# First modulation by blocks of 128 columns behind x, and the values projected first, as token rows

## The chip, the cores and the metric

The kernel runs on one core of a Trainium2 chip. The metric is the device time of one execution in microseconds (us). The engines are named as the profile names them: PE is TensorE (matmuls and transposes; PEld its weight loads), DVE is VectorE, ACT is ScalarE, POOL is GpSimd, and SP is SyncE, which only issues DMAs here. Every engine works through its own list of instructions in order and waits for the others by semaphores.

## The reference

One transformer-like block over 1024 latent tokens and 256 context tokens of width 1024, in f32. The part that the change touches is the beginning, cut to what matters:

```
mod   = silu(c)     @ w_ada + b_ada          # shift 1, scale 1, gate 1, shift 2, scale 2, gate 2
mod_c = silu(c_ctx) @ w_ada + b_ada
hc = rmsnorm(ctx, norm1_g) * (1 + csc1) + csh1
k_c, v_c = split(hc @ w_in[:, 512:1536])
h  = rmsnorm(x, norm1_g) * (1 + sc1) + sh1
q, k, v, hv, hx1, hx2, gna, ghy = split(h @ w_in)     # w_in: 1024 x 5120
y_na = neighbourhood_attention(q, k, v, k_c, v_c, rpb)
y_hy = hyena_mixer(hv, hx1, hx2, ...)        # short convolution, two long ones with computed filters
...                                           # gates, output projection, SwiGLU network, last norm
```

## The kernel before

**Products.** A product in f32 is made of three matmuls: each operand is split into a high and a low part (`split`: ScalarE casts the high part, VectorE subtracts), and low x high, high x low and high x high are summed in PSUM (`gemm`). A matmul has 128 contraction rows and streams up to 512 columns into one PSUM bank of 128 partitions.

**Opening** (`hidden`). The columns of `w_ada` for shift 1 and scale 1 (2048 of 6144) are loaded as eight slices of 128 rows, 1 MB each, in turn with x0 to x3 (128 tokens each). Each slice is multiplied as soon as it is there (line 299), with `cs`, the SiLU of c and c_ctx, as stationary operand, 32 columns wide, in the four column groups of PE; all eight accumulate in one bank. Then `ada_early` copies that bank to `msb`, transposes it and adds the biases, which gives scale and shift as columns (`mod1`). Only then can `modulated` work: for each of eight chunks of 128 channels, four transposes of normalised x (line 248), one scaling by `mod1` to `htmp` (ScalarE for even chunks, VectorE for odd ones), and the split to `hTh`, `hTl`. The normalisation (`normed`) takes squares on ScalarE, a square root (`rstd`), a reciprocal and a scaling of the x tiles. A first layer of the Hyena filters' small network (`filter_hidden`, tiles `mlp_ps`, `farg`, `feat`) is computed in the opening too, the second between the two halves of the tokens.

**Input projection** (`project`). The 40 column chunks of `w_in` (128 columns each) are the stationary operand, the transposed h moves: a chunk has two halves of 512 tokens, 24 matmuls each (line 194, tile `in_ps`), and its output has channels on partitions. Chunks 0 to 3 are q, 4 to 7 k, 8 to 11 v, 12 to 23 the Hyena input, 24 to 39 the gates. Chunks 4 to 11 are applied to the context as well (24 matmuls of 256 columns, tile `ctx_ps`). Attention needs the values v with tokens on partitions, so `tokens` transposes chunks 8 to 11 (and 12 to 23) in bank `psc` and stores them. The order is [4, 5] together, so that both run on half 0 while x4 to x7 are made ready, then one chunk after the other.

**What sets the order of work.** Instructions are written out by generators; a scheduler then orders them on each engine by readiness and priority, except for those that are pinned to program order. `_merged` mixes the projection (weight 39) with a side generator (weight `SIDE` = 496) that makes the filters, the remaining modulation rows and the long convolutions. When the side work is over, attention begins: 34 steps, each of which is followed by one half chunk of the projection (24 matmuls) as long as there is one (`left` counts the chunks), and after that by one piece of the Hyena output projection (`hy_ps`, 12 matmuls).

**Buffers.** `hT0` and `hT1` are pools for the transposed h of tokens 0 to 511 and 512 to 1023; the pool `wpool` has two buffers for split weights and one for raw ones; the filter pool `psf` has five PSUM banks; `psg` has two banks in turn, `psc` one. `stg` has two buffers for each kind of staging tile.

## Time and profile before

| what | value |
| --- | --- |
| median of three runs | 1698.57 us (1697.81 to 1703.14) |
| the profiled execution, as timed | 1693.98 us |
| its span in the trace | 1691.6 us |
| first matmul of the input projection | 37.75 us after the span's start |
| attention | about 655 to 908 us |
| PE, share of the span | 97% |
| DVE, ACT, POOL | 73%, 41%, 9% |

The span goes from the first to the last instruction of the trace; the timed execution has 2.4 us around it. The shares are means over the whole span; single stretches differ, the opening most of all. A row of the timeline has start and duration in us, the engine, the line, the operation, output and input tiles, the shape and the number of equal instructions in a row, and in brackets how long the engine had been idle before and what released it. Matmul durations overlap, so that the time from the start of one to the start of the next is what a matmul costs PE.

### The profile page before, as it was taken

Reading aid. Unit: us, or ns where it says so; the run is one execution under the profiler, and the core shown is the slowest. Engines: PE = TensorE matmul, PEld = TensorE weight load, DVE = VectorE, ACT = ScalarE, POOL = GpSimd, SP = SyncE. Lnnn points to the kernel's source line nnn. Section 1 sums busy time; section 2 is a strip of 40 time slices with the busy share of each in tenths; the row PEclk is TensorE's granted clock in tenths of the full one; section 3 lists DMA queues with packets and bytes.
Section 4 is the critical chain, followed back from the end, with each engine's and each line's share of the span. In section 5 each row is a group of like instructions: output and inputs, shape, how many; then the busy total and the mean of one; then the engine's idle time right before and its main releaser. Section 6 shows DMA issues by size and latency. Waiting matters only on the chain.

```text
span 1691.6 us, 22631 instructions
## 1 busy us (share of the span) xinstructions
PE 1645.8 (97%) x8124; PEld 1302.7 (77%) x8124; DVE 1229.1 (73%) x2076; ACT 689.6 (41%) x1206; POOL 153.3 (9%) x274
## 2 busy tenths in 40 slices
PE   6999999999999999999999999999999999999997
PEld 2777667777777787887787887888888888878886
DVE  3799587799986975565866867967865666489467
ACT  4733333222212124545654326733333334355455
POOL 0100210001000022020200001000100111000000
PEclk8999999999999999999999999999999999999999
DMA  9275662655544366344757414333422223395344
GB/s 363 96 241 194 193 215 81 209 168 172 185 169 178 124 204 182 110 140 147 218 159 256 162 62 174 119 129 121 162 92 108 94 102 123 113 359 188 100 119 155
DMA packets 110340, 274.36 MB, mean 162 GB/s; under 512 B 15503, under 2 KB 24595, under 8 KB 107925
## 3 DMA queue, kind: packets, MB, share of 16 engines
q1 hardware_dynamic: 90152, 211.86, 37.3%
q0 software_dynamic: 19280, 60.60, 10.7%
q8 instruction: 64, 1.05, 0.3%
q10 hardware_dynamic: 797, 0.45, 0.1%
q14 instruction: 47, 0.39, 0.1%
HBM read 205.48 MB, written 67.39 MB: 161 GB/s over the span
## 4 chain that ended last, share of the span: by engine, by line
PE 68%; issue 11%; DVE 5%; DMA 3%; ACT 1%; POOL 1%; SPq 0%; DVEq 0%; POOLq 0%; ACTq 0%
PE x_ps L1176 15%; PE in_ps L194 13%; PE z_ps L1176 7%; PE dx_ps L1345 6%; PE out_ps L1114 4%; PE dz_ps L1345 3%; PE dft_ps L447 2%; PE hy_ps L194 2%; PE y_ps L1176 2%; PE pt_ps L805 2%; PE pt_ps L791 2%; PE na_ps L194 2%; PE dy_ps L1345 1%; PE dft_ps L448 1%; PE dft_ps L449 1%
## 5 line engine op out<-in xcount | busy, mean ns | idle before, releaser
L194 PE MATMUL in_ps<-hTh,wl 128*128 128x512 f32 x640 | 258.4, 404 | 0.9 <-ACT proj L619 0.5
L194 PE MATMUL in_ps<-hTl,wh 128*128 128x512 f32 x640 | 252.2, 394 | 0.4 <-DVE hTl L175 0.2
L194 PE MATMUL in_ps<-hTh,wh 128*128 128x512 f32 x640 | 252.2, 394 | 0.0
L194 PEld LDWEIGHTS in_ps<-hTh,wl 128*128 128x128 f32 x640 | 120.5, 188 | 31.3 <-issue 5.3
L194 PEld LDWEIGHTS in_ps<-hTl,wh 128*128 128x128 f32 x640 | 120.6, 188 | 26.5 <-DVE hTl L175 1.9
L194 PEld LDWEIGHTS in_ps<-hTh,wh 128*128 128x128 f32 x640 | 120.5, 188 | 26.6
L175 DVE TENSOR_TENSOR wl<-wr,wh 128x1024 fp32r<-128x1024 f32 (+1 forms) x56 | 59.7, 1067 | 68.4 <-ACT wh L174 68.2
L174 ACT CAST wh<-wr 128x1024 fp32r<-128x1024 f32 (+1 forms) x56 | 51.8, 925 | 139.9 <-PE in_ps L194 112.2
L175 DVE TENSOR_TENSOR ol<-ws,oh 128x512 fp32r<-128x512 f32 x88 | 60.4, 688 | 49.1 <-ACT oh L174 49.0
L175 DVE TENSOR_TENSOR ol<-ar,oh 128x512 fp32r<-128x512 f32 x77 | 52.8, 688 | 48.0 <-ACT oh L174 48.0
L174 ACT CAST oh<-ar 128x512 fp32r<-128x512 f32 x77 | 47.9, 622 | 87.1 <-PE dx_ps L1345 33.1
L174 ACT CAST oh<-ws 128x512 fp32r<-128x512 f32 x88 | 54.7, 622 | 55.7 <-PE x_ps L1176 22.1
L780 ACT ACTIVATE pe<-pe,mx 128x640 f32<-128x640 f32 x64 | 52.6, 823 | 48.7 <-DVE mx L779 48.7
L447 PE MATMUL dft_ps<-a,matf 128*128 128x512 f32 x128 | 66.2, 598 | 4.9 <-issue 2.3
L779 DVE CUSTOM_DVE_ANT_0 pe<-s_ps,bias 128x640 f32<-128x640 f32 x64 | 50.1, 820 | 28.3 <-PE s_ps L774 28.2
L1345 PE MATMUL dx_ps<-ol,oh 128*128 128x512 f32 x176 | 68.7, 390 | 1.7 <-DVE ol L175 1.7
L1345 PE MATMUL dx_ps<-oh,ol 128*128 128x512 f32 x176 | 67.4, 390 | 1.9 <-DVE ol L175 1.9
L1345 PE MATMUL dx_ps<-oh 128*128 128x512 f32 x176 | 68.5, 389 | 0.0
L174 ACT CAST oh<-wr 128x512 fp32r<-128x512 f32 x70 | 43.3, 621 | 51.3 <-PE x_ps L1176 15.5
L175 DVE TENSOR_TENSOR ol<-wr,oh 128x512 fp32r<-128x512 f32 x70 | 48.0, 688 | 22.0 <-ACT oh L174 21.9
L1116 DVE TENSOR_TENSOR x<-x,out_ps 128x512 f32<-128x512 f32 x64 | 42.7, 684 | 16.9 <-PE out_ps L1114 16.7
L895 DVE SCALAR_TENSOR_TENSOR aacc<-wal,cs,aacc 128x512 f32<-128x512 f32 x56 | 41.8, 746 | 17.5 <-DMA wal<-in_w_ada 16.9
(396 smaller groups left out, 4215.8 us busy)
## 6 DMA issues: line engine op xcount, KB each, us to landing
wr<-in_w SPq DMA_DIRECT2D x52, 512.0 KB, 3.4
wr<-in_w_in SPq DMA_DIRECT2D x40, 512.0 KB, 4.4
ar<-g SPq DMA_DIRECT2D x77, 256.0 KB, 3.2
wal<-in_w_ada SPq DMA_DIRECT2D x64, 256.0 KB, 4.1
matf<-in_dft_f SPq DMA_DIRECT2D x32, 384.0 KB, 4.9
bias<-in_rpb SPq DMA_DIRECT2D x64, 192.0 KB, 3.7
g<-t POOLq DMA_DIRECT2D x47, 256.0 KB, 3.1
w<-in_w SPq DMA_DIRECT2D x44, 256.0 KB, 5.4
```

What stands on the lines that cost most here:

```text
L174: self.nc.scalar.copy(hi, src)
L175: self.nc.vector.tensor_sub(lo, src, hi.bitcast(F32))
L194: mm = nc.tensor.matmul(ps, ww[:, k * P:(k + 1) * P], xx[:, k, pos:pos + width], start=(i == 0), stop=(i == n - 1))
L447: nc.tensor.matmul(ps, m[:, 0], v.rearrange("p a b -> p (a b)"), start=True, stop=False)
L779: nc.vector.tensor_tensor_reduce(pe, ps[:, 256:896], bt, -1.0, 3e38, ALU.add, ALU.min, mx[:, 0:1])
L780: nc.scalar.activation(pe, pe, AF.Exp, bias=mx[:, 0:1], scale=-1.0, accum_out=mx[:, 1:2])
L791: pin(nc.tensor.transpose(pt[:, at:at + P], pe[:, c * P:(c + 1) * P], self.ident))
L895: nc.vector.scalar_tensor_tensor(acc, w, c, acc, op0=ALU.mult, op1=ALU.add)
L1114: nc.tensor.matmul(ps, gg[x][:, tk], ww[y][:, sl], start=(i == 0), stop=(i == n - 1))
L1116: nc.vector.tensor_add(x1[:, sl], x1[:, sl], ps)
L1176: mm = nc.tensor.matmul(ps, w[u][:, k * P:(k + 1) * P], x[v][:, k, :], start=(start and k == 0 and i == 0), stop=(stop and k == 3 and i == 2),
L1345: nc.tensor.matmul(ps[j], x[u][:, j * P:(j + 1) * P], w[v], start=(start and i == 0 and c == 0), stop=(stop and i == N - 1 and k == len(re ...
```

## The change

**Modulation by columns.** A new layout of the same columns, `w_ada1`, holds eight blocks; block k has all 1024 rows of the 128 shift columns and the 128 scale columns of chunk k, 1 MB each. `ada_block` multiplies one block (eight matmuls of 32x256 in the four column groups), copies the bank to `msb` (VectorE), sums the four groups with two matmuls against a selector `sel` (which leaves scale and shift as columns without a transpose), and adds the biases. It stands ahead of chunk k of the first half, so that chunk k needs block k alone. The blocks lie in the buffers of the second half's h (`h1`), two to a buffer; the loads are pinned to program order on SP, behind x0 to x3.

**Values first.** Chunks 8 to 11 leave the order; 36 chunks are left, single but for the last two. In their place a new function `opening` in `project` computes v with tokens on partitions: the transposed h is now the stationary operand and 512 columns of v's weights (`wv`, four tiles of two chunks each) move. Four banks (both of `psg`, `psc` and one of `psf`) hold 4 x 128 tokens; each chunk k adds 12 matmuls (line 690 of the changed kernel) once it is there. This is done for tokens 0 to 511, then 512 to 1023, then the 256 of the context (two banks). The banks are copied by ScalarE to `vst` (line 695) and stored. The transposes of v and of the context's v fall away, and so do the context's matmuls of chunks 8 to 11 with 256 columns, in place of which 512-column ones are half as many.

The diff at its core:

```diff
@@ _layout @@
+    out["w_ada1"] = C(A("w_ada")[0, :, :2 * D].reshape(8, P, 2, 8, P).transpose(3, 1, 0, 2, 4)).reshape(8, P, 2048)
+    out["wv"] = C(A("w_in")[0, :, 8 * P:12 * P].reshape(4, 2, P, 512).transpose(0, 2, 1, 3)).reshape(4, P, D)
@@ Block.__init__ @@
-        self.left = 40
+        self.left = 36
@@ ada_early becomes ada_block @@
+    def ada_block(self, pool, psf, w, k, cs, sel):
+        ps = psf.tile([P, 512], F32, tag="f", name="ada_ps")
+        for n in range(8):
+            j = n % 4
+            nc.tensor.matmul(ps[32 * j:32 * j + 32, 0:256], cs[:, n], w[:, n], start=(n < 4), stop=(n >= 4),
+                             tile_position=(0, 32 * j))
+        b = pool.tile([P, 256], F32, tag="msb", name="msb", bufs=2)
+        nc.vector.tensor_copy(b, ps[:, 0:256])
+        for n in range(2):
+            nc.tensor.matmul(ps[:, 256 + 2 * n:258 + 2 * n], b[:, n * P:(n + 1) * P], sel, start=True, stop=True)
+        nc.vector.tensor_scalar(self.mod1[:, :, 1, k], ps[:, 256:258], self.bcol[:, 0, k:k + 1], None, op0=ALU.add)
+        nc.vector.tensor_scalar(self.mod1[:, :, 0, k], ps[:, 258:260], self.bcol[:, 1, k:k + 1],
+                                self.ng[:, 0, k:k + 1], op0=ALU.add, op1=ALU.mult)
@@ hidden @@
+        for j in range(4):
+            load(j)
+        def block(k):
+            if k % 2 == 0:
+                w = h1.tile([P, 2, 8, 256], F32, tag="hTl" if k % 4 else "hTh", name="wada")
+                blocks.extend((w[:, 0], w[:, 1]))
+            inorder(nc.sync.dma_start(blocks[k].rearrange("p a b -> p (a b)"), a["w_ada1"][k]))
+        for k in range(4):
+            if k % 2 == 0:
+                weight(k // 2)
+            block(k)
+        weight(2)
+        normed(0, 4, "rstd1")
+        turns = [self.turned(psf, xs[0:4], 0)]
         for k in range(8):
+            self.ada_block(pool, psf, blocks[k], k, cs, sel)
+            if 1 <= k <= 4:
+                block(k + 3)
+                if k == 2:
+                    weight(3)
+            if k < 7:
+                turns.append(self.turned(psf, xs[0:4], k + 1))
+            self.chunk(pool, turns[k], 4, self.mod1[:, 0], *hT[0], k)
+            if k % 2 == 0:
...
+                self.split(*wv, raws[k // 2])
...
+            if k == 6:
+                for j in range(4, 10):
+                    inorder(load(j))
+                nc.gpsimd.dma_start(w3, a["fw3"])
+            if k < 7:
+                yield
         normed(4, 4, "rstd1b")
         next(mlp)
         yield
+        hT.append([h1.tile([P, 8, 512], F32R, tag=n, name="hT" + n[-1]) for n in ("hTh", "hTl")])
@@ project @@
+        def opening():
+            for h, n in enumerate((4, 4, 2)):
+                banks = [p.tile([P, 512], F32, tag=t, name="in_ps") for p, t in
+                         ((psg[0], "g"), (psg[1], "g"), (psc, "c"), (psf, "f"))[:n]]
+                for k in range(8):
+                    next(between)
+                    hh = hT[h] if h < 2 else hcT
+                    for j in range(n):
+                        for i, (xx, ww) in enumerate(((1, 0), (0, 1), (0, 0))):
+                            nc.tensor.matmul(banks[j], hh[xx][:, k, j * P:(j + 1) * P],
+                                             self.wv[k // 2][ww][:, k % 2], start=(k == i == 0),
+                                             stop=(k == 7 and i == 2))
+                for j, pt in enumerate(banks):
+                    st = self.stg.tile([P, 4, P], F32, tag="tm", name="vst").rearrange("p a b -> p (a b)")
+                    nc.scalar.copy(st, pt)
+                    nc.gpsimd.dma_start((self.vd if h < 2 else self.vcd)[(4 * (h % 2) + j) * P:(4 * (h % 2) + j + 1) * P], st)
@@ run @@
-                order = [[4, 5]] + [[f] for f in list(range(6, 24)) + list(range(4)) + list(range(32, 40)) + list(range(24, 30))]
+                order = [[f] for f in list(range(4, 8)) + list(range(12, 24)) + list(range(4)) + list(range(32, 40)) + list(range(24, 30))]
```

How this moves the instructions is shown at three places.

SP's queue at the program's start, before: the slices of `w_ada` (`wada`) go in turn with x0 to x3.

```order
L209 DMA cc<-in_cc 128x16
L297 DMA wada<-in_w_ada 128x2048 x2
L274 DMA x<-in_x 128x1024
L297 DMA wada<-in_w_ada 128x2048
L274 DMA x<-in_x 128x1024
L297 DMA wada<-in_w_ada 128x2048
L274 DMA x<-in_x 128x1024
L297 DMA wada<-in_w_ada 128x2048
L274 DMA x<-in_x 128x1024
L297 DMA wada<-in_w_ada 128x2048 x3
L180 DMA wr<-in_w_in 128x1024
L274 DMA x<-in_x 128x1024 x4
```

After (`wr` from `in_wv` are the raw weights of v):

```order
L213 DMA cc<-in_cc 128x16
L284 DMA x<-in_x 128x1024 x4
L318 DMA wr<-in_wv 128x1024
L314 DMA wada<-in_w_ada 128x2048 x2
L318 DMA wr<-in_wv 128x1024
L314 DMA wada<-in_w_ada 128x2048 x2
L318 DMA wr<-in_wv 128x1024
L314 DMA wada<-in_w_ada 128x2048 x2
L318 DMA wr<-in_wv 128x1024
L314 DMA wada<-in_w_ada 128x2048 x2
L284 DMA x<-in_x 128x1024 x4
L284 DMA x<-in_ctx 128x1024 x2
```

The x tiles have moved ahead of every block, the weights of v stand between the blocks, and x4 to x7 stand behind the last block as before.

ScalarE around the squares of x4 to x7, before (`junk` is the output of a square, `proj` the copy of a half chunk, `rstd1bs` the square root, `hid` the last step of the filters' network). The first row is the cast of the last chunk of half 0:

```order
L174 CAST hTh_261<-htmp_490 128x512
L174 CAST wh_496<-wr_494 128x1024
L280 ACTIVATE junk_500,ssq1_293<-x_419 128x1024
L599 COPY proj_536<-in_ps_538 128x512
L280 ACTIVATE junk_502,ssq1_293<-x_421 128x1024
L280 ACTIVATE junk_504,ssq1_293<-x_423 128x1024
L280 ACTIVATE junk_506,ssq1_293<-x_425 128x1024
L239 ACTIVATE rstd1bs_508<-ssq1_293,eps_236 128x4
L345 ACT_TABLE_LOAD
L345 ACTIVATE hid_280<-farg_516 128x1024
L599 COPY proj_537<-in_ps_564 128x512
```

After, where `hTh_260` is the cast of the last chunk of half 0, and `vst` the copy of a bank of values:

```order
L176 CAST hTh_260<-htmp_668 128x512
L289 ACTIVATE junk_672,ssq1_294<-x_628 128x1024
L289 ACTIVATE junk_674,ssq1_294<-x_630 128x1024
L289 ACTIVATE junk_676,ssq1_294<-x_632 128x1024
L695 COPY vst_714<-in_ps_290 128x512
L289 ACTIVATE junk_678,ssq1_294<-x_634 128x1024
L695 COPY vst_717<-in_ps_291 128x512
L242 ACT_TABLE_LOAD
L242 ACTIVATE rstd1bs_680<-ssq1_294,eps_236 128x4
L381 ACT_TABLE_LOAD
L381 ACTIVATE hid_277<-farg_688 128x1024
L695 COPY vst_720<-in_ps_292 128x512
```

The squares stand behind the last chunk's cast in both, with one copy of `in_ps` among them before and a copy ahead of the last square and one behind it after; a copy now waits for the whole of half 0, and a table load has come ahead of the square root.

PE at the last steps of attention, before (`s_ps` are scores, `pt_ps` the transposes of the probabilities and the products with v, `hy_ps` the pieces of the Hyena output that fill in):

```order
L771 MATMUL s_ps<-krh,qrl 128x384 x2
L771 MATMUL s_ps<-krl,qrh 128x384 x2
L771 MATMUL s_ps<-krh,qrh 128x384 x2
L774 MATMUL s_ps<-kch,ql 128x256 x2
L774 MATMUL s_ps<-kcl,qh 128x256 x2
L774 MATMUL s_ps<-kch,qh 128x256 x2
L791 MATMUL pt_ps<-ident,pe 128x128 x10
L805 MATMUL pt_ps<-pts,vc 64x128 x4
L805 MATMUL pt_ps<-pts,v 64x128 x6
L194 MATMUL hy_ps<-yhh,wl 128x512
L194 MATMUL hy_ps<-yhl,wh 128x512
L194 MATMUL hy_ps<-yhh,wh 128x512
```

After:

```order
L829 MATMUL s_ps<-kch,ql 128x256 x2
L829 MATMUL s_ps<-kcl,qh 128x256 x2
L829 MATMUL s_ps<-kch,qh 128x256 x2
L846 MATMUL pt_ps<-ident,pe 128x128 x10
L860 MATMUL pt_ps<-pts,vc 64x128 x4
L860 MATMUL pt_ps<-pts,v 64x128 x6
L846 MATMUL pt_ps<-ident,pe 128x128 x10
L860 MATMUL pt_ps<-pts,vc 64x128 x4
L860 MATMUL pt_ps<-pts,v 64x128 x6
L860 MATMUL pt_ps<-pts,vc 64x128 x4
L860 MATMUL pt_ps<-pts,v 64x128 x6
L198 MATMUL na_ps<-yah,wl 128x512
```

The filler has run out there: scores and transposes stand behind each other, up to the attention's own output projection (`na_ps`).

More of the change, by code (lines that the diff above doesn't have):

```diff
@@ L251, in modulated, with chunk, hidden @@
     def modulated(self, pool, psf, xs, n, mod, hi, lo, raw=None):
+        for k in range(8):
+            self.chunk(pool, self.turned(psf, xs, k), n, mod, hi, lo, k, raw)
+    def chunk(self, pool, pt, n, mod, hi, lo, k, raw=None):
         nc = self.nc
-        ahead, self.turns = self.turns, {}
-        for k in range(8):
-            pt = ahead[k] if k in ahead else self.turned(psf, xs, k)
-            h = raw[:, k, :] if raw is not None else pool.tile([P, 512], F32, tag="htmp", name="htmp", bufs=3)
-            if k % 2:
-                nc.vector.tensor_scalar(h[:, :n * P], pt[:, :n * P], mod[:, 0, k:k + 1], mod[:, 1, k:k + 1],
-                                        op0=ALU.mult, op1=ALU.add)
-            else:
-                nc.scalar.activation(h[:, :n * P], pt[:, :n * P], AF.Identity, bias=mod[:, 1, k:k + 1],
-                                     scale=mod[:, 0, k:k + 1])
-            self.split(hi[:, k, :], lo[:, k, :], h[:, :n * P])
-    def hidden(self, pool, wpool, mp, hid, w3, hT, hcT, psf):
+        h = raw[:, k, :] if raw is not None else pool.tile([P, 512], F32, tag="htmp", name="htmp", bufs=3)
+        if k % 2:
+            nc.vector.tensor_scalar(h[:, :n * P], pt[:, :n * P], mod[:, 0, k:k + 1], mod[:, 1, k:k + 1],
+                                    op0=ALU.mult, op1=ALU.add)
+        else:
+            nc.scalar.activation(h[:, :n * P], pt[:, :n * P], AF.Identity, bias=mod[:, 1, k:k + 1],
+                                 scale=mod[:, 0, k:k + 1])
+        self.split(hi[:, k, :], lo[:, k, :], h[:, :n * P])
+    def hidden(self, pool, wpool, h1, mp, hid, w3, hT, hcT, psf):
         nc, a = self.nc, self.a
@@ L294, in hidden @@
             nc.scalar.dma_start(getattr(self, n), a[n])
-        for k in range(8):
-            w = pool.tile([P, 2048], F32, tag="wada", name="wada", bufs=3)
-            nc.sync.dma_start(w, a["w_ada"][k, :, 0:2048])
-            for j in range(4):
-                nc.tensor.matmul(ps[32 * j:32 * j + 32, :], self.cs[:, 2 * k:2 * k + 32], w[:, j * 512:(j + 1) * 512],
-                                 start=(k == 0), stop=(k == 7), tile_position=(0, 32 * j))
-            if 1 <= k < 5:
-                load(k - 1)
-            if k == 5:
-                normed(0, 4, "rstd1")
@@ L305, in hidden @@
-        self.ready[4] = self.weights(wpool, a["w_in"][4])
-        for k in range(2):
-            self.turns[k] = self.turned(psf, xs[0:4], k)
-        self.ada_early(pool, psf, ps)
-        for j in range(4, 10):
-            load(j)
-        nc.gpsimd.dma_start(w3, a["fw3"])
-        self.modulated(pool, psf, xs[0:4], 4, self.mod1[:, 0], *hT[0])
-        self.ready[5] = self.weights(wpool, a["w_in"][5])
+        nc.vector.tensor_scalar(self.bcol[:, 1, :], self.bcol[:, 1, :], 1.0, None, op0=ALU.add)
@@ L577, in tokens, with project @@
             nc.gpsimd.dma_start(dst[:, 4 * h:4 * h + m], st[:, :m])
-    def project(self, groups, wpool, psg, psc, hT, hcT, between, then):
+    def project(self, groups, wpool, xpool, psg, psc, psf, hT, hcT, between, then):
         nc = self.nc
@@ L594, in half, with out @@
             self.gemm(pt, w, hT[h], 8, 512, 0, self.pinned)
+            out(f, st, ps, h)
+        def out(f, st, ps, h):
+            sl = slice(h * 512, (h + 1) * 512)
+            pt = ps[-1]
             if f < 4:
@@ L661, in project @@
                         yield
-                if group is groups[0]:
-                    next(between)
                 if group is groups[-1] and not h:
@@ L977, in run @@
                     with tc.tile_pool(name="x0", bufs=1, side="right") as xp:
[L978 to L979 removed]
+                        hidden = self.hidden(xp, wpool, h1, mp, hid, w3, hT, hcT, psf)
                         hyena = self.hyena_out(h0, wpool, psg[0])
[L981 removed]
+                        proj = self.project(order, wpool, xp, psg, psc, psf, hT, hcT, hidden, lambda: next(hyena))
                         next(proj)
```

77 lines of the change are left out of this document (37 added, 40 removed).

## The prediction

> **What bounds the kernel now.** I read the shares of the engines first, then the busy time by stage, then PE's own timeline of the first 75 us, and last the lists of ScalarE and VectorE beside it. The first row gives each engine's busy time, share and instructions; the next ones a stretch, its length, busy time (and instructions) of PE, PEld, DVE, ACT and POOL, the granted clock, the DMA share and GB/s.
>
> ```profile
> PE 1645.8 (97%) x8124; PEld 1302.7 (77%) x8124; DVE 1229.1 (73%) x2076; ACT 689.6 (41%) x1206; POOL 153.3 (9%) x274
> 0.00:40.00 40.00, 23.89 (x112) 8.41 (x113) 13.11 (x25) 16.08 (x24) 1.38 (x7) 0.83 0.92 363
> 40.00:80.00 40.00, 37.77 (x195) 28.27 (x194) 30.11 (x49) 32.01 (x55) 4.28 (x10) 1.00 0.25 87
> 80.00:640.00 560.00, 550.13 (x2443) 418.13 (x2443) 459.52 (x739) 159.69 (x268) 64.52 (x106) 1.00 0.54 182
> 640.00:910.00 270.00, 265.57 (x1974) 214.69 (x1973) 170.15 (x386) 143.48 (x266) 37.23 (x67) 1.00 0.52 160
> ```
>
> PE bounds the kernel: 1645.8 of 1691.6 us. Only the first 40 us leave it much room, 16.1 us idle at a clock of 0.83 with the DMA share at 0.92; there the change works. From 80 us on, PE idles 1 to 2%, so later work is worth its PE time.
>
> How that room is made up, on PE:
>
> ```profile
> 31.49 1.07 PE L299 MATMUL ada_ps<-wada,cs 128*32 128x512 f32 x8
> 37.75 0.48 PE L194 MATMUL in_ps<-hTh,wl 128*128 128x512 f32 x1
> 40.33 1.88 PE L338 MATMUL mlp_ps<-feat,mlp 128*128 128x512 f32 x4
> 48.08 0.39 PE L194 MATMUL in_ps<-hTh,wl 128*128 128x512 f32 x1
> 51.97 0.40 PE L194 MATMUL in_ps<-hTh,wh 128*128 128x512 f32 x1
> 52.78 2.66 PE L248 MATMUL hT_ps<-ident,x 128*128 128x128 f32 x20 [0.41 <-DVE x L289]
> 55.87 1.53 PE L248 MATMUL hT_ps<-ident,x 128*128 128x128 f32 x12 [0.43 <-ACT htmp L262]
> 57.16 0.71 PE L194 MATMUL in_ps<-hTh,wl 128*128 128x512 f32 x2
> ```
>
> The modulation ends at 32.6, and the first main matmul starts at 37.75. Half 0 of chunks 4 and 5 (48 matmuls) ends at 52.2, 14.4 us later; PE then waits until 57.16, but does 32 transposes meanwhile (20 in 2.66, 0.133 each, and 12). At full rate, 17 matmuls from 48.08 to 51.97 take 3.89: 0.2288 each.
>
> **The change, part by part.** *When the first main matmul starts.* ScalarE and VectorE before it:
>
> ```profile
> 15.13 0.69 DVE L344 TENSOR_SCALAR farg<-farg 128x1024 f32<-128x1024 f32 x1
> 15.91 1.06 ACT L345 ACTIVATE feat<-farg 128x1024 f32<-128x1024 f32 x1 [2.02 <-issue]
> 23.96 1.06 ACT L280 ACTIVATE junk<-x 128x1024 f32<-128x1024 f32 x1 [2.51 <-DMA x<-in_x]
> 25.13 1.28 ACT L239 ACT_TABLE_LOAD   x1
> 32.89 1.05 ACT L174 CAST wh<-wr 128x1024 fp32r<-128x1024 f32 x1
> 34.30 1.22 DVE L175 TENSOR_TENSOR wl<-wr,wh 128x1024 fp32r<-128x1024 f32 x1
> 41.66 0.78 ACT L262 ACTIVATE htmp<-hT_ps,mod 128x512 f32<-128x512 f32 x1
> 42.47 0.62 ACT L174 CAST hTh<-htmp 128x512 fp32r<-128x512 f32 x1
> 43.40 0.68 DVE L175 TENSOR_TENSOR hTl<-htmp,hTh 128x512 fp32r<-128x512 f32 x1
> ```
>
> Now x3 arrives at 23.96 (the square that waits for it), behind five 1.05 MB slices. At 0.42 MB/us (414 and 438 GB/s in the rows of 16 to 20 us further down) it comes 12.5 us earlier without them, near 11.5, and the first block and the first weights, 1.57 MB, near 15.2 (estimates). Then the program's order binds: the table load, sqrt and reciprocal on VectorE stand behind the filter MLP's chain, which ends at 15.82; so the reciprocal comes near 16.5. Behind it run the low part of the weights 1.22, a 128x1024 scaling (1.1, as a square), a table load 1.28 with its Sin 1.06, a second scaling, a cast 1.05, and the first chunk's 0.78 + 0.62 + 0.68: with the hand-overs, **24.5** (18.5 at best, if the weights' work and the Sin move out of the chain).
>
> *Values, half 0, chunk by chunk.* The modulation's matmuls at a low clock, to set beside those at 31.49:
>
> ```profile
> 26.38 1.94 PE L299 MATMUL ada_ps<-wada,cs 128*32 128x512 f32 x8 [1.75 <-DMA wada<-in_w_ada]
> ```
>
> PE has 96 × 0.2288 = 22.0; seven blocks of eight modulation matmuls at 1.07 = 7.5 (its eight 256-wide ones stream as many columns as the four 512-wide ones of a slice, which are the eight records of 1.07); 24 transposes × 0.13 = 3.1; the filter MLP's second layer 1.88, now at another place; and seven pairs of 128x2 matmuls that the trace doesn't have, between two transposes (0.26) and two 512-wide f32 ones (0.94), taken at 0.3 as small as they are: 2.1. Sum 36.6. Cold clock at its start (eight 512-wide modulation matmuls take 1.94 cold, 1.07 warm) +2.0, with 0 and 2.2 for ends, and 1.6 for waits between chunks. Half 0 ends at 24.5 + 40.2 = 64.7. The old order would have the same 96 matmuls done at 52.2 + 48 × 0.2288 = 63.2. So **+1.5**: the early start buys only what the modulation, now PE work between main matmuls, takes back. Blocks 4 and 5 share a buffer with 0 and 1 and are fetched only behind chunk 0's matmuls (about 30), and wv3, x4 to x7, the context and the next weights stand behind them on SP: 6.8 MB at 0.42 MB/us put x7 near 47, 10 us ahead of its use. I cost that at nothing; without this cover, a block late by 3 us is 3 us of PE.
>
> *Between half 0 and half 1.* This is where I see the loss. The squares of x4 to x7 stand on ScalarE behind the cast of chunk 7, and bank copies stand among them:
>
> ```profile
> 49.08 1.06 ACT L280 ACTIVATE junk<-x 128x1024 f32<-128x1024 f32 x1
> 50.27 0.30 ACT L239 ACTIVATE rstd1bs<-ssq,eps 128x4 f32<-128x4 f32 x1
> 51.16 0.17 DVE L241 RECIPROCAL rstd1b<-rstd1bs 128x4 f32<-128x4 f32 x1
> 51.88 2.74 DVE L289 TENSOR_SCALAR x<-x,rstd1b 128x1024 f32<-128x1024 f32 x4
> 52.97 0.57 ACT L599 COPY proj<-in_ps 128x512 f32<-128x512 f32 x1
> ```
>
> From a square to what follows it are 1.19 us. The cast of chunk 7 can be done about 6 us before PE is through, three squares follow, and then the copy of the first bank, which is full 9 matmuls before the end: end − 2.06. Then copy 0.58, last square 1.19, second copy 0.58, table load 1.28, sqrt 0.30, reciprocal 0.17, four scalings 2.74: end + 4.8. Then four transposes and 0.78 + 0.62 + 0.68: the first matmul of half 1 comes at end + 7.4, with 28 transposes (3.6) still to do, 11.0 against the 4.96 of before: **+6.0**. Bounds: −4.96, if all of it hides, and +8, if hand-overs double.
>
> *The clock behind this gap.* Before, transposes lie in the gap and the clock stays 1.00 (40 to 80 us). Afterwards PE has nothing for about 5 us and little for 2 more.
>
> ```profile
> 16.00:18.00 2.00, 0.37 (x4) 0.00 (x0) 0.00 (x0) 2.00 (x3) 0.00 (x0) 0.73 0.98 414
> 18.00:20.00 2.00, 0.96 (x8) 0.20 (x8) 0.00 (x0) 0.01 (x1) 0.00 (x0) 0.50 1.06 438
> 1684.00:1686.00 2.00, 0.15 (x1) 0.00 (x0) 2.00 (x5) 1.64 (x5) 0.00 (x0) 1.00 0.71 262
> 1688.00:1690.00 2.00, 0.00 (x0) 0.00 (x0) 0.00 (x0) 0.00 (x0) 0.00 (x0) 0.87 0.71 262
> ```
>
> At 16 to 18 PE was busy 0.37 of 2 us and the clock fell to 0.73, then 0.50; behind the last matmul, which ends 0.15 into 1684 to 1686, it left 1.00 only in the stretch 1688 to 1690. So this gap is at the edge. Twelve matmuls at 1.94/1.07 of 2.75 cost 2.2 more, the other end is 0; **+1.8**, by the row of 16 to 18, the nearer one. The Trainium skill, "TensorE: Matmul & The Clock Gate", section "HAM oscillation — how this bites in real kernels", speaks against such a gap: a wait that crosses the activity window throttles the array again, and the next tile starts cold. Its section "What's actually happening" gives 3.4 us for the warm-up, so half of it, 1.7, would be the estimate by the page; the trace's end shows a wait of over 3.4 us without a drop, and by that row the term would be 0.
>
> *Context and what goes away.* The third of the new copies to store waits for the store of the first (two buffers), which puts ScalarE's work on the context's 0.8 to 2 us later: **+1.5** (0 to 3). Removed: 40 transposes of the values, and half of the context's matmuls.
>
> ```profile
> 72.10 0.28 PE L194 MATMUL ctx_ps<-hcTh,wl 128*128 128x256 f32 x1
> 72.70 0.28 PE L194 MATMUL ctx_ps<-hcTh,wh 128*128 128x256 f32 x1
> 415.78 0.60 PE L574 MATMUL tm_ps<-ident,proj 128*128 128x128 f32 x4
> 416.22 1.02 PE L447 MATMUL dft_ps<-a,matf 128*128 128x512 f32 x2
> ```
>
> Five 256-wide matmuls take 0.60, 0.12 each; four transposes hold PE 0.44 to the next matmul, 0.11 each. 40 × 0.11 = 4.4; 96 × 0.12 = 11.5 gives way to 48 × 0.2288 = 11.0. **−4.9**, at PE's full worth.
>
> *Attention.* By PE's order, 16 half chunks of 24 matmuls were left as filler at the first scores, now 10; the 16 pieces of the Hyena output follow as before, so the last five iterations have none.
>
> ```profile
> 860.74 2.97 PE hy_ps L194 x12
> 867.29 2.97 PE hy_ps L194 x12
> 906.86 0.66 PE L805 MATMUL pt_ps<-pts,vc 128*64 128x128 f32 x8 [1.55 <-ACT yrow L812]
> ```
>
> In the chain of waits one iteration with a 2.97 us piece takes 6.55, so 3.58 is its own work; bare, its softmax lies open: I take 3.84 each, +1.2, and as much for the last drain, whose wait is 1.55 on ScalarE: **+2.4** (0 to 8, by a 1.55 wait in each of five). The six half chunks missing there run before, where PE is full (550.1 of 560), at their own cost, which isn't new.
>
> Sum: 1.5 + 6.0 + 1.8 + 1.5 − 4.9 + 2.4 = **+8.3**. The profiled execution took 1693.98 (span 1691.6 and 2.4 around it), so 1702.3; it lies 4.6 under the median of the runs, 1698.57. On the median's scale: **1707**.
>
> **The rivals.** *The second half's preparation hides.* If squares, sqrt and scalings of x4 to x7 run while PE still multiplies half 0, the +6.0 and the clock's +1.8 go: 1699, not slower. It decides at one point: the last square done before chunk 7's matmuls begin. For it: x4 to x7 are there 10 us ahead. Against it: ScalarE's order, with a bank copy between the third square and the fourth. Should it also start at 18.5, and the context's 1.5 go, 1707 − 7.8 − 6 − 1.5 = 1692: faster.
>
> *VectorE becomes the bound in the side stage.*
>
> ```profile
> 350.00:400.00 50.00, 50.00 (x227) 39.72 (x226) 47.62 (x81) 14.47 (x20) 6.56 (x9) 1.00 0.56 185
> ```
>
> There DVE is busy 47.6 of 50 us. Fewer transposes then free PE for nothing, and with 36 chunks merged where 40 were, the 4.4 don't show: 1711.5. Against it: PE was busy all of these 50 us.
>
> *It isn't chunk by chunk.* If each block's fetch waits until the buffer before is free, PE follows the DMA through chunks 4 to 7, about 3 us: 1710. For it: the shared buffers. Against it: 10 us of cover at 0.42 MB/us.
>
> **How the numbers follow.** A measurement of this kernel tells 0.3% from nothing, 5.1 us: 1693.5 to 1703.7. Forecast 0.45, of which 0.10 falls in that band; DVE-bound 0.10; DMA-paced 0.05; hidden 0.25 (0.20 in the band, 0.05 under it); hidden and early 0.15. Slower 0.35 + 0.10 + 0.05 = 0.50, same 0.10 + 0.20 = 0.30, faster 0.05 + 0.15 = 0.20. The likeliest case alone spans 1701 to 1714, by the ends of the gap's hand-overs, of the clock (0 to 2.2) and of attention (0 to 8). The range, 1690 to 1718, goes from the middle of the early case to the DVE case with attention's upper end; some 0.10 lies under it and 0.08 over it.
>
> **What would show it.** Right: the first values' matmul near 24.5, half 0 ended near 64.7, half 1's first matmul 7 us later with the bank copy before the fourth square, clock under 1.00 behind it, five last iterations of attention with no filler between scores and transposes. Wrong: a first matmul before 20, or after 28; a gap under 4 us; DVE waits in the side stage that PE's idle time shows; a block's DMA as the releaser of PE.

## The result and the profile after

The changed kernel takes 1720.78 us (median of four runs, 1719.36 to 1722.10) against 1699.50 for the kernel before: a ratio of 1.0122 (95% interval 1.0103 to 1.0141), 21.3 us slower. The direction was forecast, the size was not: the forecast was 8.3 us, and the time lies above the range's end, 1718.

The two profiles, cut at the same places of the program: to the filters' first matmul, to their last, from the first scores to attention's own output projection, and the network's first half. Columns as in the prediction; before:

```profile
0.00:72.90 72.90, 54.56 (x261) 31.41 (x261) 39.30 (x66) 43.82 (x70) 2.48 (x9) 0.91 0.60 237
72.90:266.80 193.90, 185.34 (x912) 140.18 (x911) 147.53 (x216) 71.67 (x141) 27.69 (x49) 0.99 0.60 196
650.70:908.50 257.80, 253.41 (x1921) 204.96 (x1920) 161.70 (x372) 139.77 (x260) 30.18 (x54) 1.00 0.51 158
1044.60:1469.20 424.60, 423.18 (x1882) 350.15 (x1880) 288.32 (x452) 175.89 (x304) 39.97 (x74) 1.00 0.33 114
```

After:

```profile
0.00:122.30 122.30, 95.33 (x483) 66.97 (x483) 52.07 (x94) 53.92 (x83) 6.19 (x15) 0.94 0.44 167
122.30:317.80 195.50, 188.20 (x863) 141.05 (x861) 152.83 (x228) 69.13 (x129) 24.89 (x47) 0.97 0.59 194
698.80:931.90 233.10, 220.66 (x1778) 179.41 (x1777) 157.83 (x370) 133.88 (x252) 28.67 (x51) 0.99 0.54 162
1068.60:1497.00 428.40, 426.99 (x1881) 350.79 (x1880) 288.92 (x452) 176.13 (x304) 39.98 (x74) 1.00 0.33 113
```

Length minus PE's busy time is its idle time: 18.3, 8.6, 4.4 and 1.4 us before, 27.0, 7.3, 12.4 and 1.4 after. The clock column shows a second loss in the first two stretches, 0.94 and 0.97 (0.91 and 0.99 before). Read in steps of 2 us up to attention's output projection (908 and 932 us), PE idles 32.2 us before and 47.6 after; what it loses by a low clock (busy time times one minus the clock) is 5.9 and 13.7; and its work at full clock is 869.9 and 870.8. So the 24 us are waits and the clock; the work didn't shrink. 4.0 more come in the network, with equal idle time: 423.2 us of busy PE became 427.0 for the same matmuls. (The spans differ by 27.4 us and the medians by 21.3: the profiled execution of before, 1693.98, lies 5.5 below the median of its runs, and that of after, 1720.83, at the median.)

PE's timeline after, the places that answer to the prediction's:

```profile
26.70 0.50 PE L690 MATMUL in_ps<-wh,hTl 128*128 128x512 f32 x1 [2.58 <-DVE hTl L177]
33.37 0.61 PE L234 MATMUL ada_ps<-sel,msb 128*128 128x2 f32 x4
33.90 1.06 PE L229 MATMUL ada_ps<-wada,csp 128*32 128x256 f32 x14
69.34 0.40 PE L690 MATMUL in_ps<-wh,hTh 128*128 128x512 f32 x1
72.54 0.30 PE L251 MATMUL hT_ps<-ident,x 128*128 128x128 f32 x1 [2.80 <-DVE x L298]
77.01 0.80 PE L690 MATMUL in_ps<-wh,hTl 128*128 128x512 f32 x1 [2.24 <-DVE hTl L177]
81.80 0.39 PE L690 MATMUL in_ps<-wh,hTh 128*128 128x512 f32 x1
82.03 3.00 PE L251 MATMUL hT_ps<-ident,x 128*128 128x128 f32 x26
104.71 0.50 PE L690 MATMUL in_ps<-wh,hTl 128*128 128x512 f32 x1 [2.28 <-DVE hTl L177]
133.61 2.62 PE L403 MATMUL filt_ps<-fw,hid 64*128 64x256 f32 x8 [2.84 <-DVE fv L410]
```

The values start at 26.7 and half 0 ends at 69.6; half 1 begins at 77.0, 7.4 us later, and its first twelve matmuls take 5.0 us instead of 2.75. At 104.7 PE waits 2.28 us for the last chunk of half 1, and at 133.6 it waits 2.84 us for the filters. The clock behind the two long waits, and ScalarE in the first of them:

```profile
69.60:77.00 7.40, 1.43 (x5) 0.55 (x4) 5.40 (x8) 6.46 (x9) 1.62 (x3) 0.86 0.43 166
77.00:82.00 5.00, 4.99 (x12) 3.94 (x13) 0.00 (x0) 0.00 (x0) 0.00 (x0) 0.53 0.04 13
128.00:144.00 16.00, 13.16 (x42) 9.16 (x41) 8.51 (x14) 8.60 (x19) 3.84 (x8) 0.68 0.77 246
67.67 0.59 ACT L695 COPY vst<-in_ps 128x512 f32<-128x512 f32 x1 [0.40 <-PE in_ps L690]
68.16 1.06 ACT L289 ACTIVATE junk<-x 128x1024 f32<-128x1024 f32 x1
```

The copy of the first bank stands between the third square and the fourth, as its order said, and waits 0.40 us for PE.

At attention's end PE has no filler. The first and the last of six waits there are shown below (a seventh, 1.55 us at 930.22, was there before the change too, at 906.86). Ahead of them stands the place where the filler changes from chunks to pieces of the Hyena output, the first two rows from the kernel before, the next two from the changed one:

```profile
799.83 0.50 PE L194 MATMUL hy_ps<-yhh,wl 128*128 128x512 f32 x1 [0.50 <-ACT proj L619]
805.38 1.32 PE L791 MATMUL pt_ps<-ident,pe 128*128 128x128 f32 x10 [1.14 <-ACT yrow L812]
793.13 1.31 PE L846 MATMUL pt_ps<-ident,pe 128*128 128x128 f32 x10 [2.83 <-ACT yrow L867]
797.65 0.50 PE L198 MATMUL hy_ps<-yhh,wl 128*128 128x512 f32 x1 [1.97 <-ACT proj L659]
905.46 1.31 PE L846 MATMUL pt_ps<-ident,pe 128*128 128x128 f32 x10 [0.56 <-ACT yrow L867]
926.11 1.31 PE L846 MATMUL pt_ps<-ident,pe 128*128 128x128 f32 x10 [1.49 <-ACT yrow L867]
```

### The profile page after: what moved, and what is told of

Its sections match the earlier page's. It is cut to its first block, busy times and chain, and to the rows that moved or that the text cites. A ratio compares the mean times of both kernels' runs of the same rounds, so it can differ in the third digit from the quotient of the medians.

```text
span 1719.0 us, 22621 instructions
## 1 busy us (share of the span) xinstructions
PE 1658.0 (96%) x8128; PEld 1312.4 (76%) x8128; DVE 1234.7 (72%) x2096; ACT 687.2 (40%) x1193; POOL 149.8 (9%) x272
## 4 chain that ended last, share of the span: by engine, by line
PE 75%; issue 10%; DVE 7%; DMA 5%; ACT 3%; POOL 0%; SPq 0%; ACTq 0%; POOLq 0%; DVEq 0%
PE in_ps L198 15%; PE x_ps L1230 15%; PE z_ps L1230 7%; PE dx_ps L1399 5%; PE out_ps L1168 4%; PE in_ps L690 3%; PE dz_ps L1399 3%; PE dft_ps L483 3%; PE hy_ps L198 3%; PE y_ps L1230 2%; PE na_ps L198 2%; PE pt_ps L846 2%; PE pt_ps L860 2%; PE dft_ps L485 1%; PE dft_ps L484 1%
## 5 line engine op out<-in xcount | busy, mean ns | idle before, releaser
L198 PE MATMUL in_ps<-hTh,wl 128*128 128x512 f32 x576 | 233.5, 405 | 1.6 <-ACT proj L659 1.6
L198 PE MATMUL in_ps<-hTh,wh 128*128 128x512 f32 x576 | 228.4, 396 | 0.0
L198 PE MATMUL in_ps<-hTl,wh 128*128 128x512 f32 x576 | 228.3, 396 | 0.0
L198 PEld LDWEIGHTS in_ps<-hTh,wl 128*128 128x128 f32 x576 | 109.2, 190 | 29.1 <-issue 4.8
L198 PEld LDWEIGHTS in_ps<-hTh,wh 128*128 128x128 f32 x576 | 109.2, 190 | 23.6
L198 PEld LDWEIGHTS in_ps<-hTl,wh 128*128 128x128 f32 x576 | 109.3, 190 | 23.3 <-issue 1.0
L1168 PE MATMUL out_ps<-wouh,ml 128*128 128x512 f32 x128 | 50.0, 391 | 0.0
## 6 DMA issues: line engine op xcount, KB each, us to landing
bias<-in_rpb SPq DMA_DIRECT2D x64, 192.0 KB, 3.8
```

Source lines behind the costliest of these rows:

```text
L198: mm = nc.tensor.matmul(ps, ww[:, k * P:(k + 1) * P], xx[:, k, pos:pos + width], start=(i == 0), stop=(i == n - 1))
L1168: nc.tensor.matmul(ps, gg[x][:, tk], ww[y][:, sl], start=(i == 0), stop=(i == n - 1))
```

## The experiments

Ratios are to the kernel before, on the same chip; "changed" is 1720.8. The rows come from several chips, on which the median of the kernel before was 1698.2 to 1700.2, so two rows are compared by their ratios where a few us matter, and a difference inside the intervals is called so.

| kernel | median us | ratio (95%) |
| --- | --- | --- |
| e1 squares ahead | 1713.4 | 1.0083 (1.0067 to 1.0100) |
| e2 filler kept for attention | 1724.4 | 1.0141 (1.0124 to 1.0157) |
| e3 both | 1717.9 | 1.0108 (1.0091 to 1.0126) |
| e4 all modulation first | 1725.0 | 1.0151 (1.0132 to 1.0170) |
| e5 blocks alone | 1718.1 | 1.0102 (1.0072 to 1.0131) |
| e12 blocks alone, chunk 5's weights earlier | 1708.2 | 1.0070 (1.0048 to 1.0092) |
| e6 values first alone | 1719.8 | 1.0116 (1.0092 to 1.0140) |
| e7 e1, block 0 ahead of x | 1711.7 | 1.0063 (1.0040 to 1.0086) |
| e8 e1, filler in pieces of 6 | 1720.6 | 1.0124 (1.0099 to 1.0149) |
| e9 e7, rates loaded early | 1711.4 | 1.0077 (1.0063 to 1.0091) |
| e10 changed, one tile at its old size | 1718.3 | 1.0117 (1.0102 to 1.0132) |
| e11 e9 with that tile | 1707.7 | 1.0054 (1.0039 to 1.0069) |
| e13 before, that tile 128 bytes longer | 1701.3 | 1.0012 (0.9996 to 1.0028) |
| e14 e11, 2 half chunks ahead of attention | 1705.1 | 1.0039 (1.0023 to 1.0055) |
| e15 e11, none ahead | 1715.2 | 1.0094 (1.0073 to 1.0115) |

### The gap between the halves (e1)

```diff
             if k == 6:
                 for j in range(4, 10):
                     inorder(load(j))
                 nc.gpsimd.dma_start(w3, a["fw3"])
+                normed(4, 4, "rstd1b")
             if k < 7:
                 yield
-        normed(4, 4, "rstd1b")
         next(mlp)
```

> Edit: the squares, square root and scalings of x4 to x7 are written ahead of chunk 7 of the first half, so that ScalarE does them while PE still multiplies the first half. Theory (the gap between the halves costs 7.4 us of waiting and 2.2 us of low clock behind it): half 1's first matmul comes within 1.5 us of half 0's last, the twelve matmuls behind it run at full rate, and the time falls by 6 to 10 us against the changed kernel, to about 1711 to 1715. Rival (what is won there is lost at the next wait, the start of the filters): half 1 starts early, but the scores of attention start less than 3 us earlier, and the time falls by less than 3 us.

PE's timeline and the clock around the end of half 0 in e1:

```profile
66.92 0.60 PE L251 MATMUL hT_ps<-ident,x 128*128 128x128 f32 x4
69.62 0.50 PE L690 MATMUL in_ps<-wh,hTl 128*128 128x512 f32 x1 [2.10 <-DVE hTl L177]
64.00:76.00 12.00, 9.90 (x47) 7.77 (x47) 10.50 (x15) 4.74 (x8) 1.96 (x4) 1.00 0.24 90
```

The first transposes of half 1 come at 66.9, ahead of half 0's last twelve matmuls, which follow at 69.6 behind a wait of 2.1 us; half 1 begins right behind them, at 72.5 in place of 77.0, and the clock stays at 1.00. The time falls by 7.4 us, clear of the intervals; by the filters' start 5.4 us of it are there (116.9 us against 122.3), by the first scores 6.1. The gap and the clock behind it are shown as a cause, at about the size that the prediction had (6.0 + 1.8).

### Filler: moving it (e2, e3) and cutting it finer (e8)

```diff
-                for _ in _merged((side(), SIDE), (proj, 39)):
+                for _ in _merged((side(), SIDE), (proj, 35)):
```

> Edit: the projection's weight in the merge with the side work is 35 in place of 39, so that it goes slower there and about 16 half chunks instead of 10 are left as filler for attention. Theory (attention without filler costs about 8 us of PE's time against before): PE's idle time from the first scores to the attention's own output projection falls from 12 us to about 4, and the time falls by 5 to 9 us, to about 1712 to 1716. Rival (the side work needs that filler as much): the idle time turns up between 146 us and the first scores instead, and the time stays within 2.5 us of the changed kernel's.

The filters, the rest of the side work, and attention in e2:

```profile
122.20:307.80 185.60, 175.63 (x809) 132.11 (x809) 148.14 (x221) 65.62 (x122) 24.23 (x46) 0.96 0.61 199
307.80:674.80 367.00, 361.00 (x1508) 272.80 (x1506) 313.80 (x532) 88.28 (x131) 43.22 (x72) 1.00 0.53 176
674.80:932.40 257.60, 253.07 (x1921) 204.98 (x1920) 161.52 (x372) 139.65 (x261) 30.38 (x54) 1.00 0.51 159
```

Attention idles 4.5 us instead of 12.4, as much as before the change. But the two stretches ahead idle 10.0 and 6.0 where the changed kernel has 7.3 and 0.9, and the time is not shorter: its median is 3.6 us longer, inside the intervals. The rival's mechanism holds: filler is short as a whole, and where it lies only decides which stage waits. The other profiles agree. Kernels with 10 half chunks left for attention (changed, e1, e4, e6 to e11) idle 9.0 to 13.2 us there, those with 16 (before, e2, e3, e5, e12, e13) 4.4 to 7.1.

> Both edits at once, the squares and the merge weight of 35. Theory (two separate places of PE's own waiting): the gains add up to 12 to 18 us, a time of 1703 to 1709. Rival (one hides the other, since work that starts earlier moves the point where attention begins): less than 11 us.

1717.9, 2.9 us under the changed kernel and 4.5 above e1: the gains do not add up, as the rival said. What e2 costs alone it seems to cost here too, but neither cost is clear of the intervals.

```diff
+                for k in range(4):
+                    for i, (u, v) in enumerate(((1, 0), (0, 1), (0, 0))):
...
+                    if k == 1:
+                        yield
-                self.gemm(ps, w, yh, 4, 512, h * 512, True)
```

> Added to the moved squares: a piece of the Hyena output as filler is 6 matmuls instead of 12, so that each of the last 22 steps of attention has one; no work is added or removed. Theory (steps with no filler lose about 1 us each): PE's idle time in attention falls from 11.7 to 5 to 8 us and the time by 3 to 6 us against the moved squares alone, to 1707 to 1711. Rival (a step needs more than 6 matmuls to be covered, and all 22 wait a little): idle time 10 us or more, time within 2 us or longer.

Attention and the stage behind it in e8:

```profile
694.90:929.00 234.10, 224.16 (x1778) 179.09 (x1777) 156.86 (x370) 133.57 (x252) 28.46 (x50) 0.99 0.54 164
929.00:1070.20 141.20, 136.93 (x609) 112.71 (x610) 104.68 (x152) 49.67 (x78) 3.73 (x7) 0.99 0.43 146
```

The rival holds, at the edge of its 10 us: idle time is 9.9 us against 11.7 in e1, PE's busy time in attention rises by 5 us (224.2 against 219.2 in e1), and the stage behind, which the last pieces now run into, takes 141.2 us (136.7 in the changed kernel). So pieces of six matmuls do not cover the steps.

### Undoing and separating the two parts (e4, e5, e12, e6)

```diff
         for k in range(8):
             self.ada_block(pool, psf, blocks[k], k, cs, sel)
             if 1 <= k <= 4:
                 block(k + 3)
...
+        for k in range(8):
             if k < 7:
                 turns.append(self.turned(psf, xs[0:4], k + 1))
```

> Edit: all eight blocks of the modulation are multiplied before the first chunk; the rest of the change stays. The blocks 4 to 7 are then fetched without waiting for chunk 0's matmuls. Theory (chunk by chunk buys nothing, since the same PE work lies in the way and the early matmuls run at a low clock): the first values' matmul comes near 38 instead of 26.7, the first half ends between 65 and 71 instead of 69.6, and the time is within 4 us of the changed kernel's. Rival (the early start is worth what it moves): the first half ends 8 us later and the time rises by 7 to 11 us.

A half miss: the scheduler still set some of the first chunks between, the first values' matmul came at 28.0, not near 38, and half 0 ended at 71.1. The median rose by 4.2 us, inside the intervals; up to the filters the clock costs 11.2 us against 5.7. Multiplying chunk by chunk is thus worth a few us at most here, not the 11 us by which the first matmul came earlier than before the change; since the edit moved only some of the blocks ahead, this is no clean test.

In e5 `hidden` keeps the blocks but yields as before, with the order `[[4, 5]] + ...`, chunks 8 to 11 and their transposes.

> One part alone: the modulation by column blocks behind x, as changed, but the projection as before the change (chunks 4 and 5 first, values as chunks 8 to 11 with transposes). Theory (the two parts hurt in different places: the blocks in the opening, the values first by taking filler away): attention idles about 4 us as before, since 16 half chunks are left; the first main matmul comes 7 to 12 us earlier than before, but the opening gains nothing by it, and the time is 0 to 8 us above the kernel before, 1699 to 1707. Rival (the blocks cause the whole loss): 15 us or more above it.

18 us, the rival's number, but in part by an accident of that kernel, which PE's timeline shows:

```profile
59.31 0.80 PE L194 MATMUL in_ps<-hTh,wl 128*128 128x512 f32 x1 [7.97 <-DVE wl L175]
```

The weights of chunk 5 were loaded on SP's queue behind the context. Attention idles 7.1 us in e5, not about 4. In e12 they go ahead of x4 to x7:

```diff
+            if k == 4:
+                self.ready[5] = self.weights(wpool, a["w_in"][5], pin=True)
...
-        self.ready[5] = self.weights(wpool, a["w_in"][5])
```

> The blocks alone again (projection as before the change), but with the weights of chunk 5 loaded ahead of x4 to x7 and not behind the context. In the first such kernel PE waited 8.0 us for them at 51 to 59 us. Theory (that wait was an accident of the order of the loads, and the blocks by themselves cost little): the wait falls under 2 us and the time by 7 to 12 us, to 1706 to 1711. Rival (the wait only moves to x4 to x7): within 4 us of 1718.

1708.2, with that wait gone. It cost 10 us by the medians and 5 by the ratios, whose intervals overlap. Of the 10 to 12 us that are left, about 4 are the network's stage (428.4 us, below). Most of the rest is in the opening, 7.5 us longer up to the filters (80.4 against 72.9), where x4 to x7 come behind the last block and their scalings end half 0's cover (the timeline of e12):

```profile
59.98 5.74 PE L249 MATMUL hT_ps<-ident,x 128*128 128x128 f32 x32 [3.28 <-DVE x L296]
```

In e6 the slices and `ada_early` stand as before the change, with `opening` behind them.

> The other part alone: the values first as token rows in four banks, but with the modulation as before (slices of 128 rows in turn with x, four transposes, then all chunks). Theory (values first takes the filler of attention, and its bank copies stand among the squares of x4 to x7): attention idles 11 to 13 us, a gap of 5 to 8 us stays between the halves, and the time is 10 to 20 us above the kernel before, 1710 to 1720, so most of the loss. Rival (the values first cost nothing by themselves): within 5 us of the kernel before.

As the theory had it: 11.0 us idle in attention and a gap of 8.1 us between the halves (69.0 to 77.15), 1719.8. Blocks alone cost 10 to 12, values alone 20, both 21, so their costs don't add. That both meet at the preparation of half 1 is a reading of the two waits (3.28 us in e12, the gap in e6), which no run tests by itself.

### Small repairs (e7, e9) and the place of a tile (e10, e13)

```diff
+        self.ada_block(pool, psf, blocks[0], 0, cs, sel)
         normed(0, 4, "rstd1")
...
-                if j % 2 and not j0:
+                if j == 1:
```

> Added to the moved squares: block 0 of the modulation is multiplied ahead of the transposes of x, and VectorE scales x3 in place of ScalarE. Theory (the first values' matmul waits for block 0's columns, which wait on PE behind transposes and x3): it comes at 24 to 25 in place of 26.7 and the time falls by 1 to 3 us against the moved squares alone, to 1710 to 1712. Rival (the next blocks or the DMA set the pace): no difference within 1 us.

The first matmul comes at 24.7 and the median is 1.7 us lower; the intervals overlap, so the size stays open. The edit does two things, block 0 ahead and x3 scaled on VectorE, and does not separate them.

```diff
+        nc.scalar.dma_start(self.rates, a["rates"][0].broadcast_to((P, 256)))
...
-            nc.sync.dma_start(rates, a["rates"][hf].broadcast_to((P, 256)))
+            if hf:
+                nc.sync.dma_start(rates, a["rates"][hf].broadcast_to((P, 256)))
```

The issue of that load on SP, before and in the changed kernel:

```profile
75.72 0.33 SPq L353 DMA_DIRECT2D rates<-in_rates  x1
125.66 0.33 SPq L389 DMA_DIRECT2D rates<-in_rates  x1
```

> Added to the moved squares and block 0 ahead: the decay rates of the filters are loaded on ScalarE's queue in the opening, not on SP's behind three loads of the projection's weights. Theory (in the changed kernel that load goes out only at 118 to 126 us, the filters' start waits 2.8 us for it and PE then runs 10 us at a low clock): the wait goes, PE's clock stays at 1.00 between 110 and 140 us, and the time falls by 4 to 8 us against the kernel without it (1711.7), to 1704 to 1708. Rival (VectorE's other work, which starts there too, is what the filters wait for): the wait stays over 2 us and the time within 2 us.

The filters' start in the kernel before, in e7, and (the last three rows) in e9:

```profile
82.54 1.86 PE L367 MATMUL filt_ps<-fw,hid 64*128 64x256 f32 x8 [1.14 <-DVE fv L374]
125.51 2.48 PE L405 MATMUL filt_ps<-fw,hid 64*128 64x256 f32 x8 [2.83 <-DVE fv L412]
125.52 1.10 PE L407 MATMUL filt_ps<-fw,hid 64*128 64x256 f32 x6 [1.19 <-DVE fv L414]
127.11 0.67 PE L407 MATMUL filt_ps<-fw,hid 64*128 64x256 f32 x2 [0.50 <-DVE fv L414]
296.23 1.13 PE L407 MATMUL filt_ps<-fw,hid 64*128 64x256 f32 x6 [2.49 <-DVE fv L414]
```

The time is a miss: the median moved by 0.2 us, and the ratios (1.0077 against 1.0063) overlap. The wait is not. At the filters' start it falls from 2.83 us to 1.19 and 0.50; the 2.49 at 296 is at the filters' end, where the kernel before waits 2.21 us at 251.78 too. The clock still falls behind it, but the stretch from the filters' first matmul to their last takes 192.0 us instead of 196.4. What is won there is lost ahead of it: the opening takes 117.7 us instead of 114.3, SP's first load of v's weights goes out at 9.0 us instead of 6.2, and the first values' matmul comes at 26.2 instead of 24.7. The three later kernels with the early load show the same (9.1 to 9.2, and 25.8 to 26.3). So the late load was part of the wait; why the early one moves SP's loads, and what the rest of the wait is, stays open.

```diff
-        self.cs = pool.tile([P, 16], F32, name="cs")
+        self.cs = pool.tile([P, 48], F32, name="cs")[:, 0:16]
```

The change had cut this tile from 192 to 64 bytes per partition.

> The changed kernel with one tile, the SiLU of c, given its old size of 192 bytes per partition in place of 64, with nothing else changed; every tile behind it lies 128 bytes further, where it lay before the change. Theory (the network's first half takes 428.2 us in the kernels with the small tile and 424.4 to 426.8 in those with the old one, because of where its tiles lie): that stage takes 423 to 427 us, and the time falls by 2 to 5 us against the changed kernel, to 1716 to 1719. Rival (the pace varies from execution to execution): the stage stays at 428 and the time within 1.5 us.

> The kernel before, with one small tile (the SiLU of c) 128 bytes per partition longer; no instruction differs, every tile behind it lies 128 bytes further. Theory (the pace of the network's first half depends on where its tiles lie, by steps of 128 bytes): the stage takes 427 to 429 us instead of 424.4 and the time rises by 2 to 5 us, to 1700 to 1703. Rival (the pace was a side effect of something else in the change): the stage stays within 1 us of 424.4 and the time within 1.5 us.

The network's first half in e10, and in e13:

```profile
1068.10:1494.20 426.10, 424.69 (x1881) 351.39 (x1880) 288.64 (x453) 176.16 (x304) 39.99 (x74) 1.00 0.33 114
1048.10:1476.50 428.40, 426.99 (x1881) 350.49 (x1880) 288.46 (x452) 176.17 (x304) 40.03 (x74) 1.00 0.33 113
```

426.1 us (424.5 in e11, which has the tile's old size too) against 428.4, and the kernel before, with 128 bytes more ahead of its tiles and no instruction changed, goes from 424.6 to 428.4. All ten kernels with the small tile take 428.4 or 428.5 us there, the six with the old one 424.5 to 427.0. The stage's pace follows the place of the tiles; that is shown, the mechanism is not. The whole time of e13 is 1.0012 (0.9996 to 1.0028), which can't be told from no change; that of e10 is 2.5 us under the changed kernel by the medians, inside the intervals.

### All repairs, and filler from the preparation (e11, e14, e15)

> All of them on the changed kernel: the squares ahead, block 0 ahead, the rates early, and the tile at its old size. Theory (each takes away a separate wait): 1700 to 1705, what is left above the kernel before being the last steps of attention without filler, 6 to 9 us of idle time. Rival (a further wait takes their place): 1708 or more.

1707.7, between the two: by the ratios, 1.0122 became 1.0054, so a little over half of the loss is undone. Attention still idles 11.4 us.

```diff
-AHEAD = 5
+AHEAD = 2
```

> On the kernel with all repairs: 2 half chunks instead of 5 are multiplied ahead of the first step of attention, so that 3 more are left as filler. Theory (steps without filler lose 1 to 1.5 us each, and the preparation before the first step needs no more than 2): idle time in attention falls by 2 to 4 us and the time by 1 to 4 us, to 1704 to 1707. Rival (the preparation waits in their place): idle time before the first scores grows by as much, time within 1 us or above.

> The same with none ahead, so 5 more half chunks left as filler. Theory: no step without filler stays but the last; idle time in the steps falls by 4 to 7 us, of which the preparation gives back 2 to 4, so the time is 0 to 4 us below the kernel with all repairs. Rival: the preparation gives back all of it or more.

The stretch ahead of the first scores, and attention, in e14 and then in e15:

```profile
308.00:676.90 368.90, 364.83 (x1535) 276.81 (x1533) 304.92 (x511) 88.37 (x129) 36.80 (x61) 1.00 0.51 172
676.90:919.20 242.30, 237.59 (x1848) 192.60 (x1848) 166.98 (x386) 137.31 (x258) 36.84 (x65) 0.99 0.57 169
311.80:678.10 366.30, 352.67 (x1482) 267.05 (x1478) 303.80 (x510) 85.36 (x125) 35.78 (x59) 0.99 0.51 172
678.10:931.60 253.50, 249.94 (x1897) 202.42 (x1897) 167.81 (x387) 139.10 (x261) 37.53 (x67) 0.99 0.54 164
```

With 2 ahead, attention idles 4.7 us and the stretch ahead 4.1 (11.4 and 0.8 in e11); the median is 2.6 us lower, inside the intervals. With none, the preparation idles 13.6 us, and more than half of what the repairs had won is lost again (1.0094). The best version with the change, 1705.1, is slower than the kernel before by 1.0039 (1.0023 to 1.0055).

## Why the prediction was right and wrong

The direction and the gap came out by the mechanism that was given. What failed is, first, the price of moved filler: "at their own cost, which isn't new" put the six half chunks that leave attention at nothing, and attention's term at +2.4, where it measured 8.0 us of waits and 1.7 of clock. Second, half 0's term, +1.5, measured +6.4. Third, three losses that have no term: the last chunk of half 1, the clock at the filters' start and the pace of the network.

**The gap, right.** "The first matmul of half 1 comes at end + 7.4": it came 7.4 us behind half 0's end, and the last scaling ended 4.8 behind it, as forecast. The bank copies are the smaller part of it: by the rows above the first waited 0.40 us, and without the two the table load would start some 1.3 us earlier (an estimate). The rest is the chain itself, which begins only behind chunk 7's cast; e1, which writes it ahead of chunk 7, takes the gap away. The clock behind it took 5.0 − 2.75 = 2.3 us (forecast 1.8). The Trainium skill, "TensorE: Matmul & The Clock Gate", section "HAM oscillation — how this bites in real kernels", says that a wait which crosses the activity window makes the next matmuls cold: the trace agrees, with a clock of 0.86 in the wait and 0.53 behind it. The other reading, by the trace's end, under which nothing would be lost, was not borne out.

**The early start, too small.** "Half 0 ends at 64.7" was 69.6, so its term is +6.4, not +1.5. The start was 2.2 us late. The terms that the prediction lists behind the reciprocal add up to 25.4 without hand-overs, so 24.5 holds only if some of them overlap; and in the trace block 0's columns waited on PE behind the transposes of x. With block 0 ahead and x3 on VectorE the start came at 24.7 (e7), later at 25.8 to 26.3 (e9, e11, e14, e15), so the share of each is open. Of the rest, a pair of selector matmuls takes PE about 0.5 us (33.37 to 33.90), not 0.3, which is 1.6 for seven, and the values' matmuls come every 0.233 us, not 0.2288, which is 0.4; some 0.7 stay open. That the early start buys nothing was right: up to the first main matmul PE idles 17.3 us (16.0 before), and the modulation, which lay in those 16 us before, now lies behind them.

**The savings, used up.** "−4.9, at PE's full worth": work at full clock rose by 0.9 instead. Eight selector pairs (4 us) and 240 matmuls at 0.0045 more (1.1 us) stand against it; the prediction had 2.1 us for seven pairs, in half 0's term, and nothing for the pace. In part this is the same excess as in half 0's term, not a further one; that the removed work itself was worth 4.9 us no run shows alone.

**Attention, too small.** "+2.4 (0 to 8)": waiting rose by 8.0 us, and the clock took 1.7. The steps without filler wait 0.4 to 1.5 us each, 4.1 together, where 2.4 was forecast. The rest lies where the forecast had nothing: at 793 and 797 PE waits 4.8 us (2.0 at the same place before), since ScalarE's copy stands behind casts that wait for loads of the Hyena output's input and of the context's keys, and behind the first scores 1.6 (0.5 before). The waits at 793 and 797 vary: in e10, whose attention has the same matmuls, one of 2.46 us is left. "At their own cost, which isn't new" is the sentence that failed: e2 and e15 show that filler taken from one stage is missed there. Chunks of the projection moved to the opening are filler lost: the opening does not wait less for them, its idle time up to the filters is 27.0 us where it was 18.3.

**Terms that weren't there.** The last chunk of half 1 has its transposes behind 72 matmuls on PE: 2.28 us and about 1.6 us of clock, to be read from the order and overlooked. The filters' start: 2.84 us (1.14 before) and 10 us at a clock of 0.5 to 0.7; no step of the prediction looked past the context. The new loss there is the clock, 6.3 us against 1.6 from the filters' first matmul to their last: PE's idle time in that stretch is lower than before, 7.3 against 8.6. By e9 the late load of the decay rates is part of the wait. The network's 4 us: no row of before could show them.

**The rivals.** The preparation of half 1 did not hide. VectorE did not bound the side work: PE idles 0.9 us there. It was chunk by chunk: no block's DMA released PE. The +1.5 at the context did not come either: from the start of half 1's last matmul to that of the context's first are 2.8 us, 3.2 before.

## What to carry to other kernels

Work that is moved into a stretch is won only if the engine that bounds the kernel idles there while that work could run: list the waits of the stretch one by one and ask which of them it fills. Independent matmuls kept for later can be worth more than their own time where later stages wait (here 144 of them, about 33 us of PE, went with 8 us of waits); count them as a stock, since taking them earlier makes the waits appear elsewhere. For each chain that a step delays (here the second half's tiles, the filters, the attention's loads) look at the first wait behind it on every engine's list, not only at the next one.

## What the hardware showed that wasn't expected

The pace of matmuls depends on where their tiles lie: with every tile behind a small one moved by 128 bytes, the same matmuls of the network's first half keep PE busy 427.0 us instead of 423.2. From one start to the next are 0.22 or 0.23 us; of some 1850 such steps 5 are 0.24 in the kernel before, 189 in the changed one, 172 in e13 and 2 in e10. Why is not shown.

The clock fell behind waits much shorter than the gap's. Behind 2.28 us at 104.71 it was 0.5 between 106 and 108 us, behind 2.84 us at the filters' start 0.68 between 128 and 144. The kernel before has this as well: behind the 2.21 us at 251.78 its clock was 0.61 and 0.53 from 252 to 256 us, while it stayed at 1.00 behind the 1.14 us at 82.54.
